# A hybrid trunk layer on one core: the state-space projection and half of the merge gates computed by seven half-size products, with all merge gates placed behind the state-space stage

## The chip, the core and the metric

The kernel runs on one core of one Trainium2 chip. The metric is the device time of one execution in microseconds (us). Three timed runs of the kernel before gave 1734.13, 1735.95 and 1740.48 us; the median is 1735.95 us.

## The reference

One layer of a trunk is applied to 1152 tokens of width 1024: a prompt of 1024 tokens, and 8 streams of 16 tokens. Cut to what matters here:

```python
h = rms_norm(x, norm_g) * (1 + scale) + shift
q, k, v, z_att, z_ssd, xbc, dt_raw, gates = split(h @ w_in)
att_branch = (attention(q, k, v) * silu(z_att)) @ w_att_proj      # 1024 -> 1024
xbc = silu(causal_dwconv(xbc))
y = ssd_scan(xs, dt, a, bm, cm) + d_skip * xs                     # 32 heads of 64, width 2048
y = grouped_rms_norm(y * silu(z_ssd)) * ssd_norm_g
ssd_branch = y @ w_ssd_proj                                       # 2048 -> 1024
g_att, g_ssd = split(gates)                                       # 1024 columns each
merged = sigmoid(g_att) * att_branch + sigmoid(g_ssd) * ssd_branch
out = x + gate * (merged @ w_out)
```

The outputs are out, the new keys and values, the last rows of the convolution and the final states of the scan.

## The kernel before, in words

Activations lie transposed: 128 channels on the partitions, 1152 tokens along the row (NT). Every fp32 operand of a large product is split into two fp16 halves, high and low, and one product is three matmuls: high by high, high by low, low by high. ScalarE writes the high half (L637 for weights, L2140 or L2116 for activations) and VectorE the low half by subtraction (L638, L2142, L2118). A third ScalarE instruction per piece (`level`, L629) sums squares for a range check whose result (`verdict`) chooses a fallback.

Two forms of dense product are used. `dense` (L858) makes 128 output channels for three groups of 384 tokens; each group sums its k-blocks of 128 in one PSUM bank (tiles d or g), and its matmuls are L873, L874 and L876 with 128x384 outputs. `quad_dense` (L764) is Strassen's scheme in Winograd's form: 256 output channels and all tokens are seen as a 2x2 block matrix with blocks of 128 channels by 576 tokens, k is taken in pairs of blocks, and seven block products stand in for eight. Each product is 24 matmuls of 128x288 outputs (L782 to L784) in a pair of PSUM banks, so one call is 168. The sums of weight blocks (`quad_split`, L661 to L664), of activation blocks (`pieces`, L2154 to L2157) and of products (`joined`, L796) are VectorE's.

The stages, in the order of the program: start-up and attention over eight head pairs; the state-space stage over 16 pairs of heads (`ssd`), in four groups of four; the merge gates that are left (`gates_dense`); the attention projection (`att_dense`, four quads); the state-space projection (`ssd_dense`: groups 0 and 1 with four k-blocks each, groups 2 and 3 together with eight), each part added into the merged tile by VectorE straight from PSUM (L2229, L2230); and the output projection (`out_dense`, four quads). I call what follows the state-space stage the tail.

In the state-space stage each pair has two plain dense products (x with its convolution, and z), and a group has two more. Then come a prelude and a main part: decays on ScalarE (L1918, L1922), masks and convolution on VectorE (L1924, L1730), small fp32 matmuls (L1965, L1993, L2000, L2013, L2038). Ten of the 16 pairs, the list GATED, have a merge gate's product behind z (`gate_dense`, L1816): 72 matmuls, three ScalarE tanh reads of PSUM (L1822) and three stores to DRAM on the POOL queue (L1823). The other six gates stand in `gates_dense`. The gates are loaded again in the tail on the SP queue (L2189).

The order on each engine is not the order in which the code is written. The code hands out instructions with generators, and then the class `Order` places all of them by a table of costs: each engine's list is fixed when the program is built. At run time each engine executes its list in order, so an instruction that waits holds up all behind it on its engine.

SBUF places are slots of a static arena: T slots of one 128x1152 fp32 tile in the tail (L_TAIL, 17 of them, and L_MORE), 3 raw weight slots (L_RAW), and half-size weight slots (L_WQ).

Of the kernel before, what the change touches and what calls it, by code (L numbers as in the profile page):

```python
# [420 lines left out]
def trunk_kernel(ctx: ExitStack, tc: tile.TileContext, h, again):  # L421
# [32 lines left out]
    for n, w in PARAMS:  # L454
# [9 lines left out]
    NPART, NOPER, NHALF = 121, 32, 32  # L464
# [34 lines left out]
                                  ("g", 3, G3)])  # L499
    L_HEAD = dict(L_SSD, T=[x for x in L_SSD["T"] if x[0] + x[1] <= Z0 + 7 * NT])  # L500
# [31 lines left out]

    blocked = [""]
    v_open = [False]
# [54 lines left out]
    gate_d = drp.tile([16, P, NT], F32, name="gate_d")  # L589

# [49 lines left out]
    def quad_split(i):  # L640
# [4 lines left out]
        try:  # L645
            for _ in range(7):
                bufs.append(alloc(L_WQ, "w", 1024))
            for _ in range(2):
                bufs.append(alloc(L_TAIL, "T", 1024))
# [4 lines left out]
        u = bufs[7:]  # L654
        del bufs[7:]
# [3 lines left out]
        t = [x.ap.rearrange("p (e k m) -> p e k m", e=2, m=P)[:, e] for x in u for e in range(2)]  # L659
        halves(bufs[0].r, bufs[1].r, w[0].ap, SW)  # L660
        nc.vector.tensor_tensor(t[0], b[0], b[1], ALU.add)  # L661
        nc.vector.tensor_tensor(t[1], t[0], a[0], ALU.subtract)  # L662
        nc.vector.tensor_tensor(t[2], a[0], b[0], ALU.subtract)
        nc.vector.tensor_tensor(t[3], a[1], t[1], ALU.subtract)  # L664
        k4 = lambda x: x.rearrange("p (k m) -> p k m", m=P)
        halves(bufs[3].r, bufs[4].r, u[0].ap, SW)
        halves(k4(bufs[2].r[:, :512]), k4(bufs[2].r[:, 512:]), b[1], SW)
        halves(bufs[5].r, bufs[6].r, u[1].ap, SW)
        for x in w:
            level(x.ap, SW)  # L670
            x.free()
        for x in u:
# [3 lines left out]
        pick = {0: (bufs[0], bufs[1], nat, 0, 0), 1: (bufs[0], bufs[1], nat, 1, 1), 2: (bufs[5], bufs[6], col, 1, 1),  # L676
                3: (bufs[2], bufs[2], col, 0, 1), 4: (bufs[3], bufs[4], col, 0, 0), 5: (bufs[3], bufs[4], col, 1, 1),
                6: (bufs[5], bufs[6], col, 0, 0)}
# [85 lines left out]
    def quad_dense(ops, evict, last=False, wide=False):  # L764

        i = widx[0]
        widx[0] += 1
        _, w = yield from w_wait(i)
        used, begun = {}, set()

        def product(q, banks, ks=range(4)):
            if q in begun:
                return
            for k in ks:
# [5 lines left out]
                for g, ps in enumerate(banks):  # L780
                    c = slice(g * HC, (g + 1) * HC)
                    nc.tensor.matmul(ps, wh, xh[:, c], start=k == 0, stop=False)  # L782
                    nc.tensor.matmul(ps, wh, xl[:, c], start=False, stop=False)  # L783
                    nc.tensor.matmul(ps, wl, xh[:, c], start=False, stop=k == 3)  # L784
                    yield 3 * 122.0
# [6 lines left out]
        def joined(t, banks, op):  # L792
            y = yield from walloc(L_TAIL, "T", HT)
            for g, ps in enumerate(banks):
                c = slice(g * HC, (g + 1) * HC)
                nc.vector.tensor_tensor(y.ap[:, c], t.ap[:, c], ps, op)  # L796
            return y

        def bank(n):
            if n % 3 == 0:  # L800
                x = pss.tile([P, 2, 512], F32, tag="s", name=nm("s"))
                return [x[:, g, :HC] for g in range(2)]
            if n % 3 == 1:
# [3 lines left out]
        b = bank(0)  # L807
        if wide:
            qs = (0, b), (1, bank(1)), (2, bank(2))
            for k in range(4):  # L810
                for q, x in qs:
                    yield from product(q, x, (k,))
            begun.update((0, 1, 2))
        yield from product(0, b)
        s1 = yield from walloc(L_TAIL, "T", HT)
        for g, ps in enumerate(b):
            nc.scalar.activation(s1.ap[:, g * HC:(g + 1) * HC], ps, AF.Copy)
        if wide:
            p3 = yield from walloc(L_TAIL, "T", HT)
# [3383 lines left out]
```

## Time and profile before

| what | value |
|---|---|
| median of three timed runs | 1735.95 us |
| span of the profiled execution, first to last instruction | 1732.7 us |
| TensorE busy, matmul records | 1706.9 us, 13977 records |
| VectorE busy | 1294.7 us (75%), 2449 |
| ScalarE busy | 982.9 us (57%), 1931 |
| mean granted TensorE clock | 0.998 |
| first scan matmul of the first and of the last pair | 695.3 and 1322.3 us |
| first quad of the attention projection / VectorE's first merge of the state-space projection / first quad of the output projection | 1366.0 / 1457.7 / 1642.0 us |
| last dense matmul | 1724.4 us |

The page gives no total for the profiled execution beside its span; the median of the timed runs lies 3.25 us above that span. A busy share is an average over stages. What bounds a stage is read from what its engines wait for, and TensorE's records overlap each other, so that the price of a matmul is the distance between starts and not its duration.

### The profile page before, as it was taken

The page shows a single profiled execution, that of the slowest core. Times are in us where ns is not written, and L with a number is a line of the kernel's source. Part 1 is how long each engine was busy: PE and PEld are TensorE (multiplying, and loading weights), DVE is VectorE, ACT ScalarE, POOL GpSimd, SP SyncE. Part 2 cuts the span into 40 slices and gives each one's busy share as a digit, 9 for nine tenths or more (in the row PEclk, how much of TensorE's full clock was granted, in tenths as well). Part 3 has the DMA queues.
Part 4 walks back from the last instruction along what each step waited for, and adds up shares of the span by engine and source line. Part 5 has one row for each costly group of instructions (what it writes and reads, how often), then busy time and mean ns, then how long its engine had stood idle before and what let it go on. Part 6 is the DMA issues. An engine that isn't in the chain of part 4 may idle for free. (4 is left out here: it accounts for less than half of the span.)

```text
span 1732.7 us, 35395 instructions
## 1 busy us (share of the span) xinstructions
PE 1706.9 (99%) x13977; PEld 1094.3 (63%) x13977; DVE 1294.7 (75%) x2449; ACT 982.9 (57%) x1931; POOL 314.4 (18%) x576
## 2 busy tenths in 40 slices
PE   7999999999999999999999999999999999999998
PEld 3556566566555566667666666666666677666676
DVE  6458767878776876587869777777777878897694
ACT  8766556566465646566556545755567543365340
POOL 0243233225134011111311231112112200000000
PEclk9999999999999999999999999999999999999999
DMA  9248789887978586445655445544556646331141
GB/s 383 80 126 206 174 229 214 183 228 192 214 210 197 150 203 140 138 137 150 150 153 155 139 134 162 169 136 118 152 174 223 252 157 226 118 127 51 53 160 71
DMA packets 276777, 287.26 MB, mean 166 GB/s; under 512 B 209069, under 2 KB 209721, under 8 KB 276601
## 3 DMA queue, kind: packets, MB, share of 16 engines
q1 hardware_dynamic: 267640, 256.26, 53.7%
q0 software_dynamic: 8960, 28.65, 4.5%
q8 instruction: 111, 1.82, 0.5%
q14 instruction: 66, 0.53, 0.1%
HBM read 192.70 MB, written 43.66 MB: 136 GB/s over the span
## 5 line engine op out<-in xcount | busy, mean ns | idle before, releaser
L873 PE MATMUL d<-arena 128*128 128x384 f16 x1872 | 610.9, 326 | 2.8 <-ACT arena L1707 1.4
L876 PE MATMUL d<-arena 128*128 128x384 f16 x1872 | 610.3, 326 | 0.0
L874 PE MATMUL d<-arena 128*128 128x384 f16 x1872 | 610.3, 326 | 0.0
L873 PEld LDWEIGHTS <-arena 128*128 128x128 f16 x1896 | 185.5, 98 | 127.6 <-issue 13.6
L876 PEld LDWEIGHTS <-arena 128*128 128x128 f16 x1896 | 185.5, 98 | 122.6
L874 PEld LDWEIGHTS <-arena 128*128 128x128 f16 x1896 | 185.6, 98 | 117.2 <-issue 3.2
L629 ACT ACTIVATE arena<-arena 128x1024 bf16<-128x1024 f32 (+4 forms) x185 | 184.9, 999 | 106.1 <-DMA arena<-in_wall_dram 64.8
L638 DVE SCALAR_TENSOR_TENSOR arena<-arena 128x1024 f16<-128x1024 f32 (+2 forms) x133 | 159.6, 1205 | 75.5 <-ACT arena L637 72.7
L637 ACT ACTIVATE arena<-arena 128x1024 f16<-128x1024 f32 (+2 forms) x133 | 135.7, 1022 | 90.8 <-DVE arena L662 18.7
L926 PE MATMUL d<-arena 128*128 128x384 f16 (+1 forms) x568 | 186.8, 329 | 0.0
L928 PE MATMUL d<-arena 128*128 128x384 f16 (+1 forms) x568 | 186.1, 328 | 0.0
L927 PE MATMUL d<-arena 128*128 128x384 f16 (+1 forms) x568 | 186.1, 328 | 0.0
L1472 ACT ACTIVATE arena<-arena 128x640 f32<-128x640 f32 (+4 forms) x144 | 100.8, 701 | 62.7 <-DVE arena L1475 62.2
L1918 ACT ACTIVATE arena<-arena 128x128 f32<-128x128 f32 x288 | 89.4, 392 | 39.5 <-DMA arena<-acs_d 38.8
L1730 DVE SCALAR_TENSOR_TENSOR arena<-arena 128x1176 f32<-128x1176 f32 x72 | 104.0, 1445 | 3.3 <-issue 1.3
L926 PEld LDWEIGHTS <-arena 128*128 128x128 f16 x576 | 56.3, 98 | 50.8 <-issue 17.5
L1508 DVE SCALAR_TENSOR_TENSOR arena<-arena 128x640 f16<-128x640 f32 (+4 forms) x128 | 86.8, 711 | 0.0
L1367 ACT ACTIVATE arena<-d 128x256 f32<-128x256 f32 x71 | 26.9, 378 | 96.4 <-PE d L928 96.4
L928 PEld LDWEIGHTS <-arena 128*128 128x128 f16 x576 | 56.4, 98 | 38.4 <-issue 0.2
L927 PEld LDWEIGHTS <-arena 128*128 128x128 f16 x576 | 56.4, 98 | 32.8
L1475 DVE CUSTOM_DVE_ANT_0 arena<-s,arena 128x320 f32<-128x320 f32 (+4 forms) x128 | 60.2, 501 | 19.8 <-PE s L1637 9.8
L1400 POOL TENSOR_SCALAR arena<-arena 128x16 f32<-128x16 f32 (+1 forms) x24 | 10.0, 417 | 353.8 <-DVE arena L1373 353.6
(267 smaller groups left out, 3051.7 us busy)
## 6 DMA issues: line engine op xcount, KB each, us to landing
arena<-in_wall_dram SPq DMA_DIRECT2D x85, 512.0 KB, 4.7
arena<-acs_d SPq DMA_DIRECT2D x32, 576.0 KB, 4.7
arena<-in_kc_dram SPq DMA_DIRECT2D x64, 256.0 KB, 4.3
arena<-in_vc_dram SPq DMA_DIRECT2D x64, 256.0 KB, 4.6
arena<-in_wada_dram SPq DMA_DIRECT2D x24, 512.0 KB, 9.4
arena<-in_xT_dram SPq DMA_DIRECT2D x16, 576.0 KB, 6.7
gate_d<-arena POOLq DMA_DIRECT2D x48, 192.0 KB, 3.7
arena<-eacs_d SPq DMA_DIRECT2D x32, 288.0 KB, 5.5
```

What stands on the lines that cost most here:

```text
L629: keep(nc.scalar.activation(junk[:, :n], x, AF.Square, scale=scale * n ** -0.5, accum_out=sums[:, c:c + 1]))
L637: keep(nc.scalar.activation(hi, x, AF.Copy, scale=scale))
L638: keep(nc.vector.scalar_tensor_tensor(lo, x, scale, hi, ALU.mult, ALU.subtract))
L873: nc.tensor.matmul(ps, hi.r[:, wc], kh.r[:, tok], start=k == 0, stop=False)
L874: nc.tensor.matmul(ps, hi.r[:, wc], kl.r[:, tok], start=False, stop=False)
L876: nc.tensor.matmul(ps, lo.r[:, wc], kh.r[:, tok], start=False, stop=k == nk - 1)
L926: nc.tensor.matmul(ps, kh.r[:, tok], wh, start=k == 0, stop=False)
L927: nc.tensor.matmul(ps, kh.r[:, tok], wl, start=False, stop=False)
L928: nc.tensor.matmul(ps, kl.r[:, tok], wh, start=False, stop=k == KT - 1)
L1472: nc.scalar.activation(p, p, AF.Exp, bias=sm_[:, 4 + e:5 + e], scale=-1.0, accum_out=sm_[:, 6 + e:7 + e])
L1730: nc.vector.scalar_tensor_tensor(yc, r.ap[:, j:j + n], w4[:, i, j:j + 1], yc, ALU.mult, ALU.add)
L1918: nc.scalar.activation(me[e].ap[:, cs], me[e].ap[:, cs], AF.Relu, scale=-1.0, bias=a4[:, c, hds[e]:hds[e] + 1])
```

## The change

The numbers of lines that follow belong to the changed kernel.

- **State-space projection.** It is now eight calls of `quad_dense`, in two passes of four: the first pass takes groups 0 and 1 (eight k-blocks, a pair of blocks at a time) and stores its result in DRAM (`acc_d`), the second takes groups 2 and 3, adds the stored result from a loaded tile, and merges.
- **Merge gates.** No gate stands in the state-space stage any more. Behind it, `gates_dense` makes eight gates by plain `dense` and the other eight by four quads, for which `h_pieces` builds block sums of the normed input.
- **Products summed in PSUM.** Products 0, 5, 6 and 3 of a quad go into one pair of banks (`fore`, without clearing in between), 4 and 2 into another (`side`). ScalarE copies an intermediate sum out (`kept`, L863), and VectorE adds 154 times from PSUM (L859, L869).
- **Weights.** `quad_split` sums in place in the raw tile, without two extra T slots; 20 quads instead of 8 use it.
- **The rest.** The attention product is stored (`att_o`) and loaded again in the second pass. Four T slots are added to the state-space stage. Loads of the tail wait until enough T slots are free (`room`). The range check of activations is taken from the fp32 blocks (576 wide) throughout.

Instructions in the built program, before and after: 1896 and 1320 of each of the three 128x384 dense matmuls, 448 and 1120 of each of the three 128x288; on VectorE 2452 and 2547 in all; on ScalarE 1605 and 1772; DMA issues on POOL 48 gate stores before, then 24 of the old size and 48 of 128x576.

```diff
-    for i in range(29, 85):
-        job(h["wall"][i])
+    NPLAIN = 8
...
+    for i in range(NPLAIN):
+        job(gate_w[i])
+    for i in range(NPLAIN, 16, 2):
+        job(gate_w[i], gate_w[i + 1], quad=True)
     for i in range(0, 8, 2):
         job(h["watt"][i], h["watt"][i + 1], quad=True)
-    for i in range(8):
-        job(h["wssd"][i])
-    for i in range(8, 12):
-        job(h["wssd"][i], h["wssd"][i + 4])
+    for i in range(0, 16, 2):
+        job(h["qssd"][i], h["qssd"][i + 1], quad=True)
...
+        yield from product(0, fore)
+        p1 = yield from kept(fore, 0, 0)
+        yield from product(4, side)
+        p5 = yield from kept(side, 1, 1)
+        yield from product(5, fore, first=False)
+        u2 = yield from kept(fore, 0, 1)
+        if not wide:
+            lone = bank(0 if odd else 2)
+        yield from product(1, lone)
+        yield from joined(0, 0, p1, lone)
...
+        yield from product(6, fore, first=False)
...
+        yield from joined(1, 1, p5, fore)
+        if not wide:
+            yield from product(2, side, first=False)
+        yield from joined(0, 1, u2, side)
...
+            yield from product(3, fore, first=False)
+            yield from evict(1, 0, [(g * HC, HC, ps) for g, ps in enumerate(fore)], None) or ()
...
-            if p in GATED:
-                yield from gate_dense()
...
-                nc.vector.scalar_tensor_tensor(t.ap, gates[8 + c].ap[:, tok], 1.0, ps, ALU.add, ALU.mult)
-                nc.vector.tensor_tensor(gates[c].ap[:, tok], gates[c].ap[:, tok], t.ap, ALU.add)
...
+                nc.vector.scalar_tensor_tensor(a.ap[:, tok], g.ap[:, tok], 1.0, a.ap[:, tok], ALU.add, ALU.mult)
+                nc.vector.tensor_tensor(m.ap[:, tok], m.ap[:, tok], a.ap[:, tok], ALU.add)
...
-    items.append((gates_dense(), [att_prep(), gate_loads()], [], 0.5))
-    items.append((att_dense(), [ssd_prep(0), mod_gate()], [], 0.5))
...
+    items.append((gates_dense(), [h_pieces(), att_prep()], [], 0.5))
+    items.append((att_dense(), [tile_loads(4, ("ga", gate_d, 0)), ssd_prep(), mod_gate()], [], 0.5))
+    items.append((ssd_dense(0), [], [], 0.5))
+    items.append((ssd_dense(1), [tile_loads(3, ("acc", acc_d, 0), ("gs", gate_d, 8), ("att", att_o, 0))], [], 0.5))
```

How the order moves at two places. ScalarE's list around the scan of the eleventh pair, before (L1888 reads z from PSUM, L1822 a gate, L1970 the scan's first block; L629 and L637 belong to a weight block, L1941 to the turn of x):

```order
L1732 ACTIVATE arena<-arena 128x1176
L1888 ACTIVATE arena<-d_12500 128x384
L1941 ACTIVATE arena<-arena 128x2304
L1888 ACTIVATE arena<-d_12534 128x384
L637 ACTIVATE arena<-arena 128x1024
L1822 ACTIVATE arena<-d_12570 128x384
L1970 ACTIVATE arena<-g_12629 128x128
L1822 ACTIVATE arena<-d_12606 128x384
```

The same pair's scan in the changed kernel's list (L1948 reads z, L1767 to L1771 the input of the next convolution, L2028 the scan's first block, L682 and L690 a weight block, L1792 the convolution):

```order
L1948 ACTIVATE arena<-d_12178 128x384
L1792 ACTIVATE arena<-arena 128x1176
L1948 ACTIVATE arena<-d_12217 128x384
L690 ACTIVATE arena<-arena 128x1024
L1767 ACTIVATE arena<-d_12252 128x384
L682 ACTIVATE arena<-arena 128x1024
L1767 ACTIVATE arena<-d_12292 128x384
L2028 ACTIVATE arena<-g_12334 128x128
L1770 ACTIVATE arena<-d_12321 128x256
```

No read of a gate stands here any more: what TensorE does around the scan is the next pair's own dense product.

VectorE's list in the last part of the state-space projection, before (L2229 and L2230 merge a product from PSUM, L2154 to L2157 and L2142 build an operand of the output projection, L638 is a weight's low half):

```order
L2229 SCALAR_TENSOR_TENSOR arena<-arena,d_17016 128x384
L2230 TENSOR_TENSOR arena<-arena 128x384
L638 SCALAR_TENSOR_TENSOR arena<-arena 128x1024
L2229 SCALAR_TENSOR_TENSOR arena<-arena,d_17043 128x384
L638 SCALAR_TENSOR_TENSOR arena<-arena 128x1024
L2230 TENSOR_TENSOR arena<-arena 128x384
L2155 TENSOR_TENSOR arena<-arena 128x576
L2156 TENSOR_TENSOR arena<-arena 128x576
L2157 TENSOR_TENSOR arena<-arena 128x576
L2142 SCALAR_TENSOR_TENSOR arena<-arena 128x1152
```

The same place in the changed kernel (L859 adds a product to the loaded first pass, L869 joins a product, L713 to L716 sum weight blocks, L2317 and L2318 merge, L2172 and L2163 build the operand):

```order
L869 TENSOR_TENSOR arena<-arena,d_17459 128x288
L869 TENSOR_TENSOR arena<-arena,d_17460 128x288
L859 TENSOR_TENSOR arena<-arena,d_17490 128x288
L2315 TENSOR_TENSOR arena<-arena 128x576
L691 SCALAR_TENSOR_TENSOR arena<-arena 128x512
L2317 SCALAR_TENSOR_TENSOR arena<-arena 128x576
L2163 SCALAR_TENSOR_TENSOR arena<-arena 128x576
L2318 TENSOR_TENSOR arena<-arena 128x576
L859 TENSOR_TENSOR arena<-arena,d_17491 128x288
L2172 TENSOR_TENSOR arena<-arena 128x576
```

The two merging instructions per product group are joined by the products' own sums and by more weight work in one list.

More of the change, by code (lines that the diff above doesn't have):

```diff
@@ L463, in trunk_kernel @@
     eps2 = fix(1)
[L464 removed]
+    NPART, NOPER, NHALF = 121, 16, 80
     sums = fix(NPART + 2 + NOPER + NHALF)
@@ L845, in quad_dense @@
+        if not wide:
+            lone = bank(0 if odd else 2)
+        yield from product(1, lone)
+        yield from joined(0, 0, p1, lone)
         w_next(i)
         if wide:
-            b = [p3.ap[:, g * HC:(g + 1) * HC] for g in range(2)]
-        else:
-            b = bank(6)
-            yield from product(2, b)
-        c = yield from joined(u4, b, ALU.add)
-        u4.free()
-        if wide:
-            p3.free()
-        yield from evict(0, 1, c) or ()
+            yield from product(2, side, first=False)
@@ new lines, in trunk_kernel, with tile_loads @@
+    tiles = {}
+    done_to = {}
+    def tile_loads(ahead, *what):
+        for name, src, at in what:
+            tiles[name], done_to[name] = [], [0]
+        for c in range(8):
+            for name, src, at in what:
+                yield from ready(lambda: c < done_to[name][0] + ahead)
+                yield from room(1 if len(what) == 1 else 0)
+                t = yield from walloc(L_TAIL, "T", NT)
+                dma(t.ap, src[at + c])
+                tiles[name].append(t)
+                yield from pause(4000 / len(what))
```

462 lines of the change are left out of this document (257 added, 205 removed).

## The prediction

> **What bounds the kernel now.** I read the page first, busy times and what the engines did; then TensorE's waits; then sums over chosen stretches; last VectorE's groups, because VectorE is the next busiest.
>
> ```profile
> span 1732.7 us, 35395 instructions
> PE 1706.9 (99%) x13977; PEld 1094.3 (63%) x13977; DVE 1294.7 (75%) x2449; ACT 982.9 (57%) x1931; POOL 314.4 (18%) x576
> ```
>
> Overlapping matmul records make "99%" weak evidence alone. The waits from 640 us to the end, by engine and releaser, settle it:
>
> ```profile
> PE d L873 <- DVE arena L1889: 1.3, 1, 1.3
> PE s L782 <- ACT arena L817: 0.8, 1, 0.8
> PE g L1855 <- ACT arena L1294: 0.5, 1, 0.5
> ```
>
> These three are all: 2.6 us in 1090. So TensorE's instruction list sets the time, and matmuls taken from it are time gained as long as the other lists keep up. Stretches of the trace, in columns stretch, length, then busy time and instructions of TensorE, weight loads, VectorE, ScalarE and POOL:
>
> ```profile
> 719.80:843.00 123.20, 123.20 (x951) 81.66 (x950) 95.83 (x146) 76.06 (x137) 16.10 (x37) 1.00 0.49 145
> 893.90:1016.20 122.30, 120.42 (x932) 79.71 (x930) 98.91 (x148) 74.70 (x136) 25.25 (x41) 1.00 0.54 151
> 1337.60:1650.20 312.60, 311.80 (x2119) 203.73 (x2118) 252.43 (x375) 153.23 (x230) 13.29 (x20) 1.00 0.41 142
> 1456.00:1556.00 100.00, 100.00 (x617) 60.21 (x616) 90.73 (x133) 51.94 (x69) 0.00 (x0) 1.00 0.45 156
> 1457.70:1642.00 184.30, 184.30 (x1136) 110.96 (x1134) 147.56 (x215) 88.49 (x129) 0.00 (x0) 1.00 0.33 110
> 1642.00:1724.60 82.60, 82.60 (x677) 65.87 (x675) 62.03 (x127) 24.11 (x39) 0.00 (x0) 1.00 0.33 115
> ```
>
> The first two are state-space stretches without a gate product; the third runs from the last VectorE add of the last pair's scan to the last operand piece of the output projection; the fourth is the densest 100 us of VectorE in the tail; the last two are plain 128x384 products and quads.
>
> **TensorE's term.** The fifth row prices a plain matmul: 184.3 us / 1136 = 0.1622 us. The sixth has 672 quad matmuls and five small ones: 82.6 / 672 = 0.1229 us. The change removes 3 x (1896 - 1320) = 1728 of the first, 280.3 us, and adds 3 x (1120 - 448) = 2016 of the second, 247.8 us. That is 32.5 us less; charging the five small ones apart makes it 34.3. I take 33.
>
> Both widths were already there, so a fixed cost per matmul can be read off: the line through 0.1229 at 288 columns and 0.1622 at 384 leaves 0.005 us at no columns, 1.4 us for 288 more matmuls, already in the prices. [...]
>
> **The end.** The last product was joined before it could be used:
>
> ```profile
> 1724.69 0.46 DVE L796 TENSOR_TENSOR arena<-arena,s 128x288 f32<-128x288 f32 x1 [1.32 <-PE s L784]
> 1725.13 0.43 DVE L796 TENSOR_TENSOR arena<-arena,s 128x288 f32<-128x288 f32 x1
> 1725.60 0.69 DVE L2308 SCALAR_TENSOR_TENSOR arena<-arena 128x448 f32<-128x448 f32 x1
> 1726.20 0.28 DVE L2311 TENSOR_TENSOR arena<-arena 128x128 f32<-128x128 f32 x1
> 1726.52 0.29 DVE L2312 TENSOR_TENSOR arena<-arena 128x128 f32<-128x128 f32 x1
> ```
>
> From 1724.69 to 1726.81 this takes 2.1 us; two 288-wide instructions from PSUM, some 0.9 us, replace it. That gains 1 us.
>
> **The state-space stage.** Ten gate products no longer lie between pairs. They gave VectorE time: TensorE worked 72 x 0.1622 = 11.7 us for a weight's low half of 1.2 us on VectorE. Without them all of the stage looks like the first two stretches: VectorE busy 78 and 81%, TensorE idle 0 and 1.9 us. Counting TensorE's list from the first to the last pair's scan gives 554 us, 4.5 such stretches: 0 to 8.5 us of idle in place of the 2 that stand there now. I take 1 us more, near the first row, because four more T slots let a pair start earlier. A gain is excluded, TensorE having hardly waited. Behind the stage eight plain gates (94 us) cover the last scans, where six (70 us) did.
>
> **The tail on VectorE, the open term.** Its groups in the third stretch (count, busy us, mean ns of one):
>
> ```profile
> L638 DVE SCALAR_TENSOR_TENSOR arena<-arena 128x1024 f16<-128x1024 f32 x32 | 38.9, 1219 | 3.4 <-ACT arena L637 2.0 <-PE d L874 1.3
> L2206 DVE SCALAR_TENSOR_TENSOR arena<-arena 128x1152 f32<-128x1152 f32 x16 | 22.5, 1412 | 3.6 <-DMA arena<-y_d 2.3 <-DMA arena<-yb 1.3
> L2218 DVE SCALAR_TENSOR_TENSOR arena<-arena 128x576 f32<-128x576 f32 x16 | 12.1, 754 | 0.2
> L796 DVE TENSOR_TENSOR arena<-arena,d 128x288 f32<-128x288 f32 x16 | 6.8, 448 | 0.0
> L2155 DVE TENSOR_TENSOR arena<-arena 128x576 f32<-128x576 f32 x6 | 4.5, 754 | 0.1
> L638 DVE SCALAR_TENSOR_TENSOR arena<-arena 128x512 f16<-128x512 f32 x6 | 4.1, 685 | 0.7 <-PE d L874 0.7
> L661 DVE TENSOR_TENSOR arena<-arena 128x512 f32<-128x512 f32 x5 | 3.4, 687 | 0.1
> ```
>
> The same stretch of the changed kernel, from the last pair's last VectorE add (L2077) to the last low half of an output operand (L2163), holds 507 VectorE instructions. Weights: 52 x 1.22 + 88 x 0.685 = 124 us. Adds from PSUM: 130 x 0.45 = 58. Low halves of operands, priced like L2206 less its second operand's 0.06 and like L2218: 54 x 1.35 + 16 x 0.75 = 85. Block differences: 72 x 0.753 = 54. Normalisation and sums of the normed input: 16 x 1.41 + 4 x 1.35 = 28. Merges with gates: 45 x 0.75 + 12 x 0.45 = 39, the rest 9. Sum 397 us of durations. Neighbours overlap:
>
> ```profile
> 1408.15 0.68 DVE L662 TENSOR_TENSOR arena<-arena 128x512 f32<-128x512 f32 x1
> 1408.76 0.68 DVE L663 TENSOR_TENSOR arena<-arena 128x512 f32<-128x512 f32 x1
> 1409.36 0.68 DVE L664 TENSOR_TENSOR arena<-arena 128x512 f32<-128x512 f32 x1
> 1409.96 1.41 DVE L2206 SCALAR_TENSOR_TENSOR arena<-arena 128x1152 f32<-128x1152 f32 x1
> ```
>
> Starts lie 0.61 us apart at 0.68 us each, so some 0.08 us an instruction comes off: 397 - 41 = 356 us. TensorE's list in the same stretch, up to the first matmul that uses that last operand, is 147 x 0.1622 + 2769 x 0.1229 + 7 (small products) = 371 us. Before, VectorE needed 252 of 313 us; now it needs 356 of 371, 96%. TensorE no longer has a safe lead: VectorE may idle 15 us.
>
> What it idled for before, in that stretch, longest sums first:
>
> ```profile
> DVE arena L2229 <- PE d L876: 28.8, 22, 7.3
> DVE arena L796 <- ACT arena L817: 9.4, 3, 3.4
> DVE arena L796 <- PE s L784: 5.1, 3, 2.1
> DVE arena L2229 <- PE g L876: 3.7, 1, 3.7
> DVE arena L2206 <- DMA arena<-y_d: 2.3, 1, 2.3
> DVE arena L638 <- PE d L874: 2.0, 3, 0.7
> DVE arena L638 <- ACT arena L637: 2.0, 2, 1.5
> DVE arena L2142 <- ACT arena L2140: 1.6, 4, 0.7
> DVE arena L796 <- PE g L1011: 1.3, 1, 1.3
> ```
>
> Idle was 312.6 - 252.4 = 60 us. The waits on PE, 41 us, shrink to nothing where VectorE is behind, as its products then lie ready. The others were some 17 us, over 375 instructions; over 507 they are 23. So the stretch takes 356 + 23 = 379 us, TensorE waiting 8. Bounds: no wait at all (VectorE never idle), and 45 (all 60 us stay: 356 + 60 - 371).
>
> **The rest, at nothing.** ScalarE gets 167 more instructions of 0.3 to 1.2 us, some 100 us on 983, 64% of the time. Stores on POOL's queue go from 48 to 72 on an engine at 18%. The queue SP carries 19 more loads and stores; a transfer that waits for a slot holds up the weights behind it, and quad sums now keep the raw tile until its last half is out. If that cover went, each late weight would cost VectorE a landing of a few us; it is part of the 23. New DRAM traffic is 32 tiles of 0.59 MB, 19 MB, over a tail that moved 110 to 156 GB/s (last column above), where the state-space stage ran as much and more without a wait.
>
> **Sum.** Against the execution profiled: 1732.7 - 33 - 1 + 1 + 8 = 1707.7 us of span. The median of the runs lies 3.25 us above that span, so 1711 us. About 0.5% (8.7 us) is what a measurement here can tell from no change.
>
> **Rivals.**
>
> *VectorE packs no better than it ever did (0.20).* Its densest 100 us of the tail were 90.7% busy. 356 / 0.907 = 392 us, 21 us of waiting: 1735.95 - 34 + 1 + 21 = 1724 us, with 1718 to 1738 around it. For it: an order fixed in advance has no play left at 96%. Against: that share was taken while TensorE set the pace.
>
> *Lock step, slower than before (0.11).* Products 5, 6 and 3 add into banks that must first be read, and the reader ahead of product 3 is VectorE, which in one list also carries operands and weights. If VectorE then waits for TensorE as often as before, while TensorE waits for VectorE, all 60 us of idle stay: 45 us of waiting, 1735.95 - 34 + 1 + 45 = 1748 us. It decides from VectorE idle of 15 + 33 = 48 us in the stretch upwards; over 0.5% slower from 57. For it: VectorE did idle 60. Against: the order puts products of the next quad between, and 41 of the 60 were TensorE's pace.
>
> *The state-space stage pays (0.10).* Every gate-free stretch idles like the second: 8.5 us instead of 1, 1718 us.
>
> *Matmuls cost by number, not by columns (0.01).* A fixed cost near 33 / 288 = 0.115 us each would eat the gain, leaving 1735.95 - 1 + 1 + 8 = 1744 us; the rows give 0.005. [...]
>
> **Numbers.** My own case, tail waits of 0 to 16 us, has 0.58 and spans 1702 to 1718. Of the packing rival two thirds lie below 1727.3 (0.13), the rest within 0.5%. Lock step splits evenly: within 0.5% and slower, 0.055 each. Faster 0.58 + 0.10 + 0.13 = 0.81; same 0.07 + 0.05 = 0.12; slower 0.06 + 0.01 = 0.07. For eight in ten the range takes my case, the stage rival and most of the packing rival: 1700 (the 34.3 us price, no waits) to 1731.
>
> **What would show it.** Right: quad matmuls still 0.122 us apart; VectorE busy near 1380 us in all and above 92% from the last scan to the last output operand; TensorE's waits there 3 to 16 us in all, on VectorE (adds from PSUM, low halves), and next to none in the state-space stage. Wrong: quad starts further apart; more than 9 us of TensorE idle between the first and the last scan; VectorE idle of 50 us or more in the tail with TensorE idle beside it, the sign of lock step.

## The result, and the profile after

The changed kernel takes 1748.12 us (median of 4 runs, 1746.5 to 1750.2) against 1735.34 us of the kernel before beside it: a ratio of 1.0071, with a 95% interval of 1.0058 to 1.0083. It is slower by 0.7%. The prediction was 1711 us, range 1700 to 1731.

The page's first lines, to be held against those of before:

```profile
span 1748.4 us, 36400 instructions
PE 1687.2 (96%) x14265; PEld 1126.0 (64%) x14265; DVE 1379.0 (79%) x2544; ACT 1064.5 (61%) x2130; POOL 348.7 (20%) x600
```

TensorE's busy time fell by 20 us and the span grew by 16. TensorE's waits from 640 us to the end were three rows and 2.6 us before; now they are fifteen rows and 34.8 us, of which the first six are:

```profile
PE g L844 <- ACT arena L690: 6.3, 3, 2.5
PE s L844 <- ACT arena L863: 6.3, 4, 4.3
PE g L846 <- DVE arena L691: 5.3, 4, 2.2
PE s L844 <- DVE arena L859: 3.5, 2, 1.9
PE g L844 <- DVE arena L859: 2.8, 1, 2.8
PE g L1352 <- DVE arena L2111: 2.0, 1, 2.0
```

The reader should see that no single line owns the loss: weights (L690, L691), copies out of PSUM (L863) and adds (L859) share it, on ScalarE and VectorE alike. Stretches of the changed kernel (stretch, length, then busy time and instructions of TensorE, weight loads, VectorE, ScalarE, POOL; granted clock, DMA share, GB/s):

```profile
695.00:1245.00 550.00, 547.13 (x4306) 365.11 (x4304) 450.88 (x689) 335.64 (x622) 125.88 (x200) 1.00 0.53 152
1273.30:1356.00 82.70, 82.52 (x675) 65.70 (x673) 71.90 (x98) 67.28 (x126) 11.77 (x21) 1.00 0.55 183
1356.00:1675.00 319.00, 287.26 (x2234) 219.57 (x2232) 273.85 (x392) 182.23 (x322) 18.35 (x34) 0.96 0.54 189
1675.10:1736.90 61.80, 61.80 (x507) 49.43 (x505) 36.52 (x81) 16.64 (x33) 0.00 (x0) 1.00 0.27 92
1273.30:1736.90 463.60, 431.68 (x3411) 334.78 (x3409) 382.37 (x570) 266.14 (x480) 30.13 (x55) 0.97 0.51 175
1249.90:1669.10 419.20, 387.28 (x3005) 293.96 (x3004) 363.70 (x509) 264.06 (x475) 39.04 (x67) 0.97 0.54 186
```

The state-space stage (first row) loses 2.9 us of TensorE's time. The four gate quads (second row) and the last three quads (fourth row) lose nothing. All of the loss lies in the third row: the attention projection, the state-space projection and the first quad of the output. VectorE is never full there (273.85 of 319 us), and the clock reads 0.96 instead of 1.00.

I price the loss by the fifth row, from the first quad matmul to the last: 3360 matmuls at 0.1229 us are 412.9 us, so 463.6 us hold 50.7 us of something else. Some 4 us of that are small fp32 products, the rest, 47 us, is waiting and slow running. Each experiment below is read by the same difference.

What VectorE waited for in the stretch that the prediction priced (the sixth row):

```profile
DVE arena L2163 <- ACT arena L2161: 14.2, 10, 5.1
DVE arena L691 <- ACT arena L690: 11.7, 9, 3.0
DVE arena L2249 <- DMA arena<-y_d: 9.8, 6, 3.5
DVE arena L2249 <- DMA arena<-yb: 4.6, 1, 4.6
DVE arena L713 <- DMA arena<-in_watt_dram: 3.0, 1, 3.0
DVE arena L859 <- PE s L846: 2.5, 1, 2.5
```

Its waits for TensorE have shrunk to almost nothing, and in their place it waits for ScalarE's high halves (14.2 + 11.7 us). ScalarE in turn waits for VectorE and for weights in the same stretch:

```profile
ACT arena L682 <- DVE arena L2318: 34.4, 9, 5.4
ACT arena L690 <- DMA arena<-in_qssd_dram: 26.1, 8, 8.1
ACT arena L863 <- PE g L846: 20.1, 11, 4.9
```

One wait shows how the two lists catch each other. The chain of waits ahead of 1661 us, start and length of each piece:

```profile
1654.44 0.67 DVE arena L2317
1655.11 0.67 DVE arena L2163
1655.78 0.68 DVE arena L2318
...
1656.53 0.79 ACT arena L682 x2
...
1657.34 0.69 ACT arena L682 x2
1658.03 2.19 ACT arena L2161 x2
1660.22 0.61 ACT arena L863 x2
...
1660.87 0.40 PE s L844
```

TensorE waits 4.3 us for L863, a copy of a product out of PSUM that takes 0.61 us. In ScalarE's list that copy stands behind range checks (L682) and two high halves (L2161), and the first check waits for VectorE's merge (L2318), which itself stands behind an operand's low half (L2163). None of the three engines is full; the time goes in handing over.

### The profile page after: what moved, and what is told of

Read it like the earlier page. It is cut to its first block, busy times and chain, and to the rows that moved or that the text cites. A ratio compares the mean times of both kernels' runs of the same rounds, so it can differ in the third digit from the quotient of the medians.

```text
span 1748.4 us, 36400 instructions
## 1 busy us (share of the span) xinstructions
PE 1687.2 (96%) x14265; PEld 1126.0 (64%) x14265; DVE 1379.0 (79%) x2544; ACT 1064.5 (61%) x2130; POOL 348.7 (20%) x600
## 4 chain that ended last, share of the span: by engine, by line
PE 68%; DVE 15%; ACT 8%; DMA 5%; issue 3%; POOL 0%; SPq 0%; DVEq 0%; ACTq 0%; POOLq 0%
PE d L933 10%; PE d L936 10%; PE d L934 10%; PE d L986 5%; PE d L987 5%; PE d L988 5%; PE g L1592 2%; DVE arena L691 2%; ACT arena L682 2%; DVE arena L2163 2%; PE g L2023 2%; PE s L2051 2%; DMA arena<-in_qssd_dram 1%; PE d L846 1%; PE d L844 1%
## 5 line engine op out<-in xcount | busy, mean ns | idle before, releaser
L933 PE MATMUL d<-arena 128*128 128x384 f16 x1320 | 431.0, 327 | 1.4 <-ACT arena L1767 1.4
L936 PE MATMUL d<-arena 128*128 128x384 f16 x1320 | 430.3, 326 | 0.0
L934 PE MATMUL d<-arena 128*128 128x384 f16 x1320 | 430.3, 326 | 0.0
L682 ACT ACTIVATE arena<-arena 128x1024 bf16<-128x1024 f32 (+4 forms) x217 | 199.2, 918 | 127.8 <-DMA arena<-in_wall_dram 68.2
L691 DVE SCALAR_TENSOR_TENSOR arena<-arena 128x1024 f16<-128x1024 f32 (+2 forms) x157 | 180.4, 1160 | 51.0 <-ACT arena L690 50.5
L690 ACT ACTIVATE arena<-arena 128x1024 f16<-128x1024 f32 (+2 forms) x157 | 154.2, 994 | 56.2 <-DMA arena<-in_qssd_dram 26.1
L844 PE MATMUL d<-arena 128*128 128x288 f16 x440 | 126.4, 287 | 1.4 <-ACT arena L2161 1.4
L845 PE MATMUL d<-arena 128*128 128x288 f16 x440 | 126.4, 287 | 1.1 <-DVE arena L2163 1.1
L846 PE MATMUL d<-arena 128*128 128x288 f16 x440 | 126.5, 287 | 0.0
L844 PE MATMUL s<-arena 128*128 128x288 f16 x360 | 103.6, 288 | 11.6 <-ACT arena L863 6.3
L844 PE MATMUL g<-arena 128*128 128x288 f16 x320 | 94.8, 296 | 11.2 <-ACT arena L690 6.3
## 6 DMA issues: line engine op xcount, KB each, us to landing
arena<-in_wada_dram SPq DMA_DIRECT2D x24, 512.0 KB, 10.2
```

Of the source, the lines that this page charges most:

```text
L682: keep(nc.scalar.activation(junk[:, :n], x, AF.Square, scale=scale * n ** -0.5, accum_out=sums[:, c:c + 1]))
L690: keep(nc.scalar.activation(hi, x, AF.Copy, scale=scale))
L691: keep(nc.vector.scalar_tensor_tensor(lo, x, scale, hi, ALU.mult, ALU.subtract))
L844: nc.tensor.matmul(ps, wh, xh[:, c], start=first and k == 0, stop=False, skip_group_check=not first)
L845: nc.tensor.matmul(ps, wh, xl[:, c], start=False, stop=False, skip_group_check=not first)
L846: nc.tensor.matmul(ps, wl, xh[:, c], start=False, stop=k == 3, skip_group_check=not first)
```

## The experiments

The lines are those of the changed kernel; in e1, e2, e7 and e15 the same code stands a few lines further up or down. "First to last quad" is the stretch of TensorE's quad matmuls, "over the price" what lies over 0.1229 us per quad matmul in it (some 4 us of small products in each), "VectorE" its busy time there.

| run | median us | ratio to before | 95% interval | first to last quad | over the price | VectorE |
|---|---|---|---|---|---|---|
| the change | 1748.12 | 1.0071 | 1.0058 to 1.0083 | 463.6 | 50.7 | 382.4 |
| e1 fourth raw slot | 1751.17 | 1.0088 | 1.0071 to 1.0105 | 462.1 | 49.2 | 382.3 |
| e2 no weight sums | 1708.65 | 0.9844 | 0.9827 to 0.9860 | 422.5 | 9.6 | 334.8 |
| e3 all gates plain | 1752.38 | 1.0091 | 1.0074 to 1.0108 | 372.8 | 42.4 | 294.4 |
| e4 ten gates back | 1759.05 | 1.0128 | 1.0109 to 1.0147 | 377.2 | 46.8 | 305.9 |
| e5 sums behind the halves | 1727.76 | 0.9951 | 0.9935 to 0.9966 | 443.8 | 30.9 | 383.0 |
| e6 sums on POOL | 1766.86 | 1.0181 | 1.0164 to 1.0198 | 478.6 | 65.7 | 390.2 |
| e7 no range check of blocks | 1728.13 | 0.9953 | 0.9936 to 0.9969 | 443.9 | 31.0 | 381.7 |
| e9 operands first | 1733.82 | 0.9986 | 0.9975 to 0.9996 | 448.5 | 35.6 | 381.1 |
| e10 weights first | 1745.00 | 1.0045 | 1.0028 to 1.0061 | 462.6 | 49.7 | 383.0 |
| e11 both first | 1726.38 | 0.9947 | 0.9931 to 0.9962 | 441.5 | 28.6 | 381.5 |
| e12 both first, gates plain | 1749.33 | 1.0070 | 1.0053 to 1.0087 | 367.8 | 37.4 | 294.8 |
| e13 flag early | 1747.57 | 1.0069 | 1.0054 to 1.0084 | 466.9 | 54.0 | 382.3 |
| e14 both first, flag early | 1726.05 | 0.9939 | 0.9926 to 0.9953 | | | |
| e15 e14, fourth raw slot | 1724.12 | 0.9938 | 0.9923 to 0.9953 | 442.9 | 30.0 | 382.3 |

(e3, e4 and e12 have 2688 quad matmuls, 330.4 us. e14 has times alone: its profiled execution took 9731.84 us, and the median is that of the other five.)

**e1, late weights.**

```diff
-        while not hold[0] and loaded[0] < len(parts) and len(wraw) < 3:
-            b = alloc(L_RAW, "raw", 1024)
+        while not hold[0] and loaded[0] < len(parts) and len(wraw) < 4:
+            try:
+                b = alloc(L_RAW, "raw", 1024)
+            except NoSlot:
+                try:
+                    b = alloc(L_HH, "T", 1024)
+                except NoSlot:
+                    return
```

> One raw weight slot more in the tail (four for three; the fourth lies where the normed input was). Theory W, late weights: the changed kernel's chain of waits between 1356 and 1669 us holds 34 us of weight loads (25.8 and 8.3) that could only start when the last low half had left the slot; with a slot more they start a quad earlier, and 15 to 30 of the 47 us of TensorE's waiting go: 1718 to 1733 us. Theory V, VectorE's amount of work: VectorE is busy 253.5 of 289 us between 1372 and 1661, as long as TensorE's own list of some 248 us, so a load that comes earlier finds VectorE no freer: 1744 to 1750 us, VectorE's wait for loads replaced by other waits. Theory R, ScalarE's range checks ahead of the operands: no change, 1746 to 1750 us.

The loads did come earlier. ScalarE's wait for them over the same stretch (1249.9 to 1669.1 us), 26.1 us in the change, is one row of 4.4 us:

```profile
ACT arena L696 <- DMA arena<-in_qssd_dram: 4.4, 1, 4.4
```

The time did not fall (1751 against 1748, over the price 49.2 against 50.7). The chain of waits had named those loads, and taking them out brought nothing: other pieces filled their place. Theory W fell, for the weights' loads.

**e2 and e5, the weight sums.** In e2 the four sums are left out; in e5 they stand behind the last halves:

```diff
-        nc.vector.tensor_tensor(a[0], a[0], b[0], ALU.subtract)
-        nc.vector.tensor_tensor(b[0], b[0], b[1], ALU.add)
-        nc.vector.tensor_tensor(b[1], b[1], a[0], ALU.subtract)
-        nc.vector.tensor_tensor(a[1], a[1], b[1], ALU.subtract)
         halves(bufs[3].r, bufs[4].r, w[1].ap, SW)
         halves(bufs[5].r, bufs[6].r, w[0].ap, SW)
```

> Leaves out the four VectorE sums of weight blocks in every quad (the products are then of wrong operands; every matmul, load and store stays). VectorE has 80 instructions of 0.61 us less, 49 us, of which 12 quads or 29 us lie in the attention and state-space projections. Theory V: waiting falls by about those 29 us and by half of the 10.6 us that TensorE ran at half clock: 1710 to 1720 us. Theory W: the sums also stand between a weight's load and its low halves, 2.4 us a quad, so half as much: 1726 to 1738 us. Theory R: no change, 1744 to 1750 us.

> The four sums of weight blocks of every quad stand behind the low halves in the raw tile instead of ahead of them (the products are of wrong operands). VectorE's work is that of the change, but the sums no longer lie on the way from a weight's load to its matmuls. Theory VA, the amount of VectorE's work: as slow as the change, 1743 to 1752 us. Theory VC, the length of the chain to a weight's low halves: as fast as without the sums, 1706 to 1716 us.

The stretch from first to last quad in e2, then in e5:

```profile
1272.50:1695.00 422.50, 418.56 (x3412) 330.95 (x3409) 334.75 (x491) 264.66 (x480) 31.01 (x55) 1.00 0.55 191
```

```profile
1272.10:1715.90 443.80, 426.29 (x3411) 333.81 (x3409) 383.03 (x571) 266.03 (x482) 29.52 (x55) 0.98 0.52 183
```

Without the sums 41 of the 50.7 us are gone, the clock is back at 1.00 and the kernel takes 1709 us, just under theory V's span: TensorE's term of the prediction is real and is reached once nothing makes it wait. With the sums back on VectorE but behind the halves, half of it returns: VectorE's busy time is that of the change (383.0), and the time is 1728. So the loss of 39.5 us that hangs on the sums splits into about 20 us for their place ahead of the halves and 19 us for their amount. Neither VA (1743 to 1752) nor VC (1706 to 1716) held alone. VectorE's other late loads, the scan's output (rows y_d and yb, 14.4 us in the change), were not tried by themselves; e2 still waits 12.0 us for them while no more than 9.6 us lie over the price, so they are not the loss by themselves.

**e3 and e4, the placing of the gates.** e3 makes all gates plain behind the stage, e4 puts ten back behind z of their pairs:

```diff
-    NPLAIN = 8
+    NPLAIN = 16
...
             st["z"] = z
+            if p in GATED:
+                yield from gate_dense()
```

(The second hunk is e4's alone.)

> All 16 merge gates as plain products behind the state-space stage, the state-space projection by quads as in the change. TensorE's list grows by 576 x 0.1622 - 672 x 0.1229 = 10.8 us. Theories W and R: the waits lie in the attention and state-space projections, where nothing is changed: 1748 + 11 = 1757 to 1761 us. Theory V: VectorE loses the sums and differences of four quads (some 70 us of work) ahead of the attention projection and can lead by what the T slots hold, a few us: 1750 to 1757 us.

> Ten gates back behind z of the ten pairs that had them, the other six plain behind the stage, the state-space projection by quads as in the change. TensorE's list is 10.8 us longer than in the change, as in the run before this. All theories that put the loss in the tail: 1755 to 1762 us, with TensorE's 3.4 us of waiting in the state-space stage gone. If the placing of the gates were the loss (rival: the state-space stage pays), this run would lie below the change: under 1745 us.

e4 came at 1759, where every theory of the tail had it; the state-space stage was not what the change lost by. It is also 6.7 us slower than e3, whose TensorE list is as long. In the two profiles e4's first quad starts 1.0 us earlier (1368.1 against 1369.1 us) and its quads take 4.4 us more, so that difference too lies mostly behind the stage. e3 at 1752 lies inside theory V's span: 10.8 us more of TensorE's list cost 4.3 us.

**e6, POOL in VectorE's place.** The four sums are issued by `nc.gpsimd`.

> The four sums of weight blocks of every quad on POOL instead of VectorE, at their place in the chain; the result is the reference's. VectorE has 49 us less, the chain to a weight's low halves is as long or longer. Theory VA: 1708 to 1722 us. Theory VC: 1745 us or more, and more the longer POOL takes for a sum of 128x512 (unknown; from VectorE's 0.61 us to some 2 us).

It is the slowest of all. POOL's sums (line, form, count, busy us, mean ns), and two of VectorE's groups in the same stretch, in e6:

```profile
L713 POOL TENSOR_TENSOR arena<-arena 128x512 f32<-128x512 f32 x19 | 30.1, 1584 | 129.9 <-ACT arena L682 68.4 <-DVE arena L2163 18.8 <-DMA arena<-in_qssd_dram 15.9
```

```profile
L2163 DVE SCALAR_TENSOR_TENSOR arena<-arena 128x1152 f16<-128x1152 f32 x50 | 81.5, 1635 | 7.9 <-ACT arena L2161 7.6 <-PE g L846 0.3
L2174 DVE TENSOR_TENSOR arena<-arena 128x576 f32<-128x576 f32 x17 | 19.8, 1162 | 0.5
```

and the same two in the change:

```profile
L2163 DVE SCALAR_TENSOR_TENSOR arena<-arena 128x1152 f16<-128x1152 f32 x50 | 67.4, 1350 | 11.5 <-ACT arena L2161 11.3
L2174 DVE TENSOR_TENSOR arena<-arena 128x576 f32<-128x576 f32 x17 | 12.9, 757 | 0.5
```

A sum of this line takes POOL 1.58 us (those of the other three 1.57 to 1.75) against VectorE's 0.68 in the change, and VectorE's own instructions are longer in the mean: 1.64 for 1.35 us, 1.16 for 0.76. The trace shows that it is the ones beside a POOL sum: of the 50 instructions of L2163, 27 overlap one and take 1.88 us, and the 23 that don't take 1.35. Adds with one input from PSUM (L869) take 0.44 us either way (39 and 91 of them). VectorE gave up 80 instructions and is busier than before (390.2 against 382.4 us). So the run says little between VA and VC; it says that this move frees nothing.

**e7, e9, e10, e11, ScalarE's range checks.** e7 leaves out the 80 checks of the activation blocks. e9 moves 64 of them behind the first halves (the 16 of the gate quads' input stay; first hunk), e10 does so with the checks of the weights (second hunk), e11 does both:

```diff
-        for x in quarters(ta, tb):
-            level(x, scale, kind="h")
         got[0], = yield from halved(ta.ap[:, :HT], HT, scale)
         got[1], got[2] = yield from halved(tb.ap[:, :NT], NT, scale)
+        for x in quarters(ta, tb):
+            level(x, scale, kind="h")
...
-        for x in w:
-            level(x.ap, SW)
         halves(bufs[0].r, bufs[1].r, w[0].ap, SW)
         halves(k4(bufs[2].r[:, :512]), k4(bufs[2].r[:, 512:]), b[1], SW)
+        for x in w:
+            level(x.ap, SW)
```

> Leaves out the range check of the activation blocks in the tail (80 ScalarE instructions of 128x576, some 0.4 to 0.8 us each; their sums are set to a constant). Theory R: the chain of waits between 1356 and 1669 us holds 20 us of L682, and ScalarE's high halves stand behind them; 10 to 25 us of waiting go: 1722 to 1738 us. Theory VA: VectorE's list is unchanged, 1740 to 1749 us.

> In the tail's operand pieces the four range checks of a pair of blocks (ScalarE, 128x576) stand behind the first three halves instead of ahead of them; the work and the result are those of the change. Theory H (handing over: TensorE waits for chains that go from ScalarE to VectorE and back through two lists in fixed order, so each step ahead of a half counts, even on an engine that is busy 57%): leaving the checks out gave 20 us, and moving them takes them out of the way of three of the seven halves but puts them before the block differences, so about half: 1734 to 1744 us. Theory VA (VectorE's amount alone): 1745 to 1751 us.

> In every quad the two range checks of the weights (ScalarE, 128x1024, 1.05 us each) stand behind the first two pairs of halves instead of ahead of them; the work and the result are those of the change. Theory H: the first products of a quad get their weights 2 us earlier, the sums wait for the checks as before: 1738 to 1746 us. Theory VA: 1745 to 1751 us.

> Both moves of the two runs before this together. Theory H: 1728 to 1742 us, better than either alone; a version that beats the kernel before only if it comes under 1727 us. Theory VA: 1745 to 1751 us.

e11, from first to last quad:

```profile
1275.20:1716.70 441.50, 423.95 (x3411) 332.23 (x3409) 381.49 (x569) 265.54 (x479) 30.07 (x55) 0.99 0.53 184
```

e7 lies where theory R had it, and e9 (1733.8) and e11 (1726.4) a little below theory H's spans, far from VA's; e10 (1745.0) stands where the two spans touch and tells nothing alone. The checks cost 20 us on an engine that is busy 57% of the stretch (266.14 of 463.6). Moving them, with every instruction kept, gives 14 us (e9), and with the weights' checks 22 us (e11), although the weights' move alone gives 3. In e11 VectorE's wait for operand halves, 14.2 us in the change, is 2.2 us in the same kind of stretch (1250 to 1690 us):

```profile
DVE arena L691 <- ACT arena L690: 11.9, 10, 3.7
...
DVE arena L2163 <- ACT arena L2161: 2.2, 6, 0.7
```

e11 does the work of the change and beats the kernel before by 0.5% (0.9931 to 0.9962). Every edit also makes `Order` place a new list. The runs with the smallest effects (e1, e10, e13) stay within 3 us of the change, so 14 to 22 us is more than a new list did in those; e12, next, shows that lists can differ by more.

**e12, e11 with plain gates.**

> Both moves, and all 16 gates plain behind the stage. TensorE's list is 10.8 us longer, the four gate quads with their sums and differences are gone. In the change that swap cost 4 us (1752 against 1748). Theory H: the same 4 us over the run before this, 1732 to 1746 us. Theory VA: 1749 to 1755 us.

A miss: 1749 us, 23 us over e11 and not 4, only 3 us under e3. The longer list accounts for 10.8 us, and 8.8 us more lie over the price (37.4 against 28.6). Counted from a quad's first matmul to the next quad's, 15.5 us over the price lie in one quad, the first of the state-space projection. e3, without the moves, loses 15.9 us in the same quad and e11 2.8: where all gates are plain, the moves did nothing for this wait. Its cause stays open.

**e13 to e15, the end, and late weights once more.** e13 is the change with

```diff
-                if c == 6 and (o, t) == (0, 1):
+                if c == 6 and (o, t) == (0, 0):
                     verdict()
```

e14 is e11 with it, and e15 adds e1's slot.

> The change, with the small instructions that decide the range check written one block of the last quad's results earlier. In the change VectorE writes the flag 0.06 us behind its last sum, at 1738.17 us, then all engines branch on it, and the span ends 10.2 us later; before, the flag came 1.6 us ahead of the last sum and the span ended 5.9 us behind that sum. If the flag holds the end: 2 to 4 us less than the change, 1744 to 1746 us, and 8 to 9.5 us from the start of the last matmul to the end. If the last stores hold it: 1747 to 1749 us, 11.4 us as before.

> Range checks of operands and of weights behind the first halves, and the flag earlier. The two effects lie at different places and should add: 1726 less 2 to 4 us, 1722 to 1724 us, if the flag holds the end; 1725 to 1728 us if not.

> The run before this with a fourth raw weight slot. If late loads are what is left of TensorE's waiting (VectorE and ScalarE still wait for some weight loads): 5 to 15 us less than the run before this, 1708 to 1718 us. If not: within 4 us of it, since a changed list alone moved the change by up to 3 us.

VectorE's last instructions in the change:

```profile
1737.61 0.51 DVE L2397 SCALAR_TENSOR_TENSOR arena<-d,arena 128x288 f32<-128x288 f32 x1
1738.03 0.14 DVE L2381 TENSOR_SCALAR again<-g 1x1 int32<-1x1 f32 x1
```

and in e13:

```profile
1740.11 0.14 DVE L2381 TENSOR_SCALAR again<-g 1x1 int32<-1x1 f32 x1
...
1743.86 0.94 DVE L2397 SCALAR_TENSOR_TENSOR arena<-d,arena 128x288 f32<-128x288 f32 x2 [0.80 <-PE d L846]
```

With the flag early, the last quad matmul starts 8.9 us before the end of the span in e13 and 6.6 in e15, against 11.5 in the change and 11.4 in e11; all the profiles of the changed kernel with the flag late have 11.2 to 11.5. So the flag held the end, by 2.6 and 4.8 us; why these two differ stays open. The whole time did not fall with it: e13 (1747.6) and e14 (1726.1, not clear of e11's 1726.4) lie in the spans that were given for an end held by the stores. e13's runs spread from 1746.7 to 1754.6, and 54.0 us lie over the price in the profiled one, so what a changed list moves elsewhere is as large as this effect. e15 is within 4 us of e14: late weight loads are not what is left, the second time that they were tried.

**e8, the clock by itself.** Behind the end of the kernel before, bursts of matmuls wait for chains of VectorE instructions:

```diff
+    x = base[:, H0:H0 + 512]
+    x16 = x.bitcast(F16)
+    for n in 3 * tuple(range(2, 15)):
+        ps = psd.tile([P, HC], F32, tag="d", name=nm("d"))
+        for j in range(100):
+            nc.tensor.matmul(ps, x16[:, :P], x16[:, P:P + HC], start=j == 0, stop=j == 99)
+        for _ in range(n):
+            nc.vector.tensor_scalar(x, x, 1.0, None, ALU.mult)
```

> The kernel before with 39 bursts of 100 matmuls of 128x288 behind its end, each burst waiting for a chain of 2 to 14 VectorE instructions of some 0.5 us, the series run three times. If idle time alone halves TensorE's clock: above one length of idle time, between 2.5 and 4.5 us by the change's trace (3.0 us once without, 4.4 us with), the first matmuls of a burst start 0.24 us apart for some 5 us, below it 0.123 us apart. If the half clock came of something else in the tail (PSUM, the loads): 0.123 us after every wait.

Two bursts: one behind 2.07 us of idle time (from 1771.5), one behind 3.91 us (from 1836.5); the column behind POOL is the granted clock:

```profile
1771.50:1777.50 6.00, 6.00 (x49) 4.81 (x50) 0.00 (x0) 0.00 (x0) 0.00 (x0) 1.00 0.00 0
...
1836.50:1841.50 5.00, 5.00 (x22) 3.15 (x23) 0.00 (x0) 0.00 (x0) 0.00 (x0) 0.50 0.00 0
1841.50:1846.50 5.00, 5.00 (x39) 3.90 (x38) 0.00 (x0) 0.00 (x0) 0.00 (x0) 0.92 0.02 3
```

49 matmuls in 6 us, then 22 in 5 us. In these rows ScalarE and POOL do nothing and the DMA share is at most 0.02: idle time alone did it. By idle time, counted from start to start less 0.123 us:

| idle us | bursts | with matmuls at half clock | length of the slow part, us |
|---|---|---|---|
| 1.15 to 2.07 | 9 | 0 | |
| 2.53 | 3 | 3 | 3.3 to 3.5 |
| 2.99 | 3 | 2 | 3.3 to 3.5 |
| 3.45 to 6.68 | 23 | 23 | 2.6 to 5.7 |

Up to 2.07 us was free in all 9 bursts, from 3.45 us on it cost in all 23, and between them the length alone doesn't tell. I had read 2.5 to 4.5 us from the change; it begins lower.

The clock records of the same trace tell the rest. The stretches of half clock behind the bursts begin whole multiples of 3.413 us apart (9, 14, 20, 25 of them behind the first, and so on), and all but the last, which runs to the end, last 3.41 or 6.83 us: in this trace the clock changed on a grid of 3.41 us. What told the waits apart is how much idle time fell into one step of this grid. Two of the waits of 2.99 us, step by step:

```profile
1797.88:1801.29 3.41, 2.51 (x21) 1.76 (x18) 0.83 (x2) 0.00 (x0) 0.00 (x0) 1.00 0.00 0
1801.29:1804.70 3.41, 1.49 (x13) 1.19 (x14) 1.73 (x5) 0.00 (x0) 0.00 (x0) 1.00 0.02 5
1804.70:1808.11 3.41, 3.41 (x30) 2.74 (x28) 0.00 (x0) 0.00 (x0) 0.00 (x0) 1.00 0.00 0
...
2029.98:2033.39 3.41, 0.58 (x6) 0.33 (x5) 2.56 (x6) 0.00 (x0) 0.00 (x0) 1.00 0.00 0
2033.39:2036.80 3.41, 3.41 (x17) 2.16 (x15) 0.00 (x0) 0.00 (x0) 0.00 (x0) 0.50 0.00 0
```

The first wait is split over two steps (1.07 and 1.92 us) and costs nothing; the second lies in one, and the next step runs at half clock. All 38 waits divide so: with at most 2.01 us of idle time in any one step the clock stayed full, with 2.5 us or more it halved, and of two waits with 2.07 us in a step one halved it.

## Why the prediction was wrong

**TensorE's term, 33 us less: right.** The last quads run 504 matmuls, with three small ones, in 61.8 us, 0.1226 us each against 0.1229 priced, and e2 reached 1709 us when the waits went.

**The state-space stage, 1 us more than the 2 before: right.** 2.9 us of waiting, inside 0 to 8.5. e4, with the gates back, was no faster.

**The end, 1 us gained: wrong, by 4 us.** From the start of the last quad matmul to the end of the span 8.4 us (1724.4 to 1732.7) became 11.5 (1736.9 to 1748.4). The step counted the adds of the last product, and these did get shorter: the last sum ended 2.4 us behind the start of the last quad matmul before and ends 1.2 us behind it now. It did not count the flag that VectorE writes next to them, 1.6 us ahead of the last sum before, 0.06 us behind it now: from the last sum to the end 5.9 us became 10.2.

**The tail, 8 us of waiting: wrong, and this is the loss.** It was 47, slow running included; in the stretch that the prediction priced it was 419.2 - 371 = 48. Two of its parts held: VectorE's busy time in the stretch (356 predicted, 363.7 measured), and its waits on TensorE, which did shrink to some 5 us. The step that failed was "The others were some 17 us, over 375 instructions; over 507 they are 23". VectorE idled 419.2 - 363.7 = 55.5 us. Its waits on anything but TensorE came to 48 us in place of 23: 27.6 on ScalarE, 19.4 on loads, 1.2 on issue. The waits on ScalarE and on loads were scaled by the number of VectorE's instructions, as though each had a fixed price. But before, TensorE's lead covered a late half and the wait cost nothing; with the lead gone an instruction ahead of a half, on either list, can move TensorE. e7, e9 and e11 show it for ScalarE's checks, e5 for the sums' place. The companion step, "ScalarE gets 167 more instructions ... 64% of the time", at nothing, failed with it: the share was foreseen well (61%) and says nothing about how long one result takes to come through. The work that was named as cover, TensorE's lead, was the very thing that the sum had used up.

**A cost that the sum did not have: the half clock.** In the change's tail 76 quad matmuls start 0.225 to 0.25 us apart, which makes 8.9 us in all over 0.123 us each; these are part of the 47. The clock stands at 0.50 in five stretches of 3.41 or 6.83 us, 27.3 us together, where the text put on record for e2 has 10.6. The rows, behind 5 us with little work and behind a wait of 3.0 us:

```profile
1486.00:1491.00 5.00, 4.92 (x21) 3.14 (x22) 5.00 (x9) 1.40 (x3) 0.69 (x2) 0.50 0.70 216
...
1640.00:1645.00 5.00, 5.00 (x43) 4.00 (x41) 5.00 (x8) 1.89 (x4) 0.00 (x0) 1.00 0.69 234
```

In e8 idle time did this by itself (22 matmuls in 5 us behind 3.91 us of it). The five stretches of the change lie on a grid of 3.41 us as those of e8 do (24, 29, 43 and 80 steps behind the first). In e8 2.07 us of idle time in one step sufficed once. In the change, the wait of 3.0 us fell on both sides of 1637.9 us, where a step begins, with 1.9 us the larger part, and cost nothing; the half clock from 1467.2 us on came behind two waits of 1.4 and 1.1 us in one step. My estimate from e8's slow parts of 2.6 to 5.7 us at half clock: a wait that puts more than some 2 us into one step costs half of such a part, 1.3 to 2.9 us, over what the waits view gives for it.

**The rivals.** "Lock step" gave 1748 us, and its sign was seen: VectorE idle of more than 50 us with TensorE idle beside it. Its mechanism was another. It had VectorE waiting for TensorE, with the reader ahead of product 3 as the place; VectorE waited some 5 us for TensorE, and the ring that closed was between VectorE and ScalarE. A number that agrees is no proof of its story. "VectorE packs no better" was right in kind and too kind in size: it took 90.7% for the stretch, which reached 86.8% (363.7 of 419.2). That share is no ceiling that VectorE has, since e11 moved only ScalarE's checks and gained 22 us; it is a sign of the handing over. Of the signs that were named, the quads' spacing and VectorE's 1379.0 us in all (1380 forecast) came out right, and VectorE's share and TensorE's waits in the tail did not. The rival on matmuls by number is out: the prices held (0.1226 us for a quad matmul, 0.1229 priced).

What stays open: why the first quad of the state-space projection costs some 16 us in e3 and e12, which of the remaining 25 us in e11 is VectorE's amount and which the order, and what of the run-to-run spread of e13 belongs to the clock.

## What to carry to other kernels

Where a change eats the lead of the engine that sets the time, add up the chain that one result goes through, instruction by instruction in each engine's list, and not the engines' busy shares: ScalarE at 57% cost 20 us with instructions that nobody waited for. Put bookkeeping (range checks, copies, flags) behind the instruction that the next engine waits for; here that alone, with no work removed, turned 0.7% slower into 0.5% faster. Take a piece of the chain of waits for a cause only when its removal moves the time: the late weight loads were 34 us of the chain, a fourth slot made them early twice (e1, e15), and it brought 2 us at most.

## What the runs showed of the hardware that I had not expected

In e8 TensorE's clock changed on a grid of 3.41 us. Behind a step with 2.5 us or more of idle time it halved for one or two steps, with at most 2.01 us in any step it stayed full, and of two waits with 2.07 us in a step one halved it; matmuls of 288 columns then started 0.24 us apart instead of 0.123, for 2.6 to 5.7 us. In e6 adds of 128x512 on POOL took 1.57 to 1.75 us in the mean of their line, and VectorE's low halves of 128x1152 (L2163) took 1.88 us beside such an add and 1.35 without; the adds that read PSUM (L869) took 0.44 us either way. And with the flag on which all engines branch written last, 11.2 to 11.5 us passed from the last matmul's start to the end, against 8.9 and 6.6 with the flag early.
